# Building a quarter of the low weight parts with an accumulating DMA in a split-precision decoder block

## The chip, the cores and the metric

The kernel runs on one core of a Trainium2 chip. The metric is the device time of one execution in microseconds (us). Three executions of the kernel before took 811.44, 811.97 and 812.96 us, so the median is 811.97 us.

## What is computed

The reference is one residual decoder layer on 256 tokens of width 2048, all in float32. Cut to what matters here:

```python
h = rms_norm(x, g_mix)
u, z_ssm, c_q, k, v, z_attn, k_idx, w_idx, gate_ssm, gate_attn = split(h @ w_in)
o_ssm  = (s5_scan(u) * silu(z_ssm)) @ w_ssm_out
o_attn = (topk_attention(c_q, k, v, k_idx, w_idx) * silu(z_attn)) @ w_attn_out
x = x + (sigmoid(gate_ssm) * o_ssm + sigmoid(gate_attn) * o_attn) @ w_o
x = x + sigmoid(rms_norm(x, g_ple) @ w_ple_gate) * rms_norm(p @ w_ple, g_ple_post)
return rms_norm(x, g_final)
```

Nearly all of the work is matrix products of the 256 token rows with large weight matrices, which are read once from HBM.

## The kernel before, in words

A float32 product is made from three products of reduced-precision operands (type float32r). Each operand is split into a high part (the value rounded) and a low part (the value minus its high part), and the kernel adds high x high, high x low and low x high in PSUM. For the activations this is done once per stage. For the weights it is done for each piece as it comes in.

The weights come in **units** of 128 partitions x 1024 columns (512 KB; eight units of the v/key projection have 672 columns). There are 256 units, numbered 0 to 255, and the main loop takes one per step. For each unit:

- `issue_unit` (L88) loads it from HBM into a tile `raw` by a DMA on the SP queue (L99). There are 5 `raw` buffers (L94), so a load has to wait until the unit five before it has been used up.
- `unit_hi` (L243) makes `hi`, the rounded copy, on ACT (L252). There are 4 `hi` buffers.
- `unit_lo` (L255) makes `lo = raw - hi` on DVE (L264). There are 4 `lo` buffers.
- TensorE then does 24 matmuls of 256 columns or 12 of 512 columns with `hi` and `lo` (L142).

At step s the loop issues the matmuls of unit s, then `hi` of unit s+3, then whatever work was deferred to this step, then `lo` of unit s+2, then the load of the next unit not yet loaded (unit s+5), and then `pump` (L229) lets generator threads run up to a budget. Since four buffers are in turn, `hi` and `lo` of unit u reuse the buffers of unit u-4 and cannot start before the matmuls of unit u-4 are done. Five units are loaded ahead of the loop by `first_loads` (L112).

Beside the units, threads do the rest of the layer. Those that matter below:

- `s5_tables` (from L754) and `s5_powers` (L732) prepare tables for the state-space branch. GpSimd (POOL) does 49 small products of 128x32 (L738 to L744) and six large ones of 128x1024 (L775 to L777); DVE does large products at L767 to L771. In the program text the POOL work stands behind the last of the DVE products.
- `s5_gen` (from L820) runs the scan on DVE, with matmuls into the PSUM tile `aux`.
- `attn_gen` does indexer, top-k and attention.

POOL otherwise computes a few small powers for the norms and a few masks. It issues no DMA. The framework sets all semaphores itself and also orders the instructions of each engine by a plan of its own, so that an engine's order can differ from the program text: the memset of `kb` (L805), which stands late in the text, is among the first things POOL runs.

Of the kernel before, what the change touches and what calls it, by code (L numbers as in the profile page):

```python
# [10 lines left out]
F32R = mybir.dt.float32r  # L11
I32 = mybir.dt.int32
AF = mybir.ActivationFunctionType
ALU = mybir.AluOpType
# [4 lines left out]
P = 128  # L19
# [14 lines left out]
XLAG = 1  # L34
ULATE = 4
TRLAG = 2

C_U, C_ZS, C_CQ, C_K, C_V, C_ZA, C_KI, C_GS, C_GA = 0, 1024, 2048, 2560, 2816, 3072, 4096, 4176, 6224

# [5 lines left out]
def block_kernel(ctx: ExitStack, tc: tile.TileContext, A: dict, out: bass.AP):  # L45
    nc = tc.nc
    V, S, G, PE = nc.vector, nc.scalar, nc.gpsimd, nc.tensor
# [3 lines left out]
    wp = ctx.enter_context(tc.tile_pool(name="wp", bufs=4))  # L51
# [8 lines left out]
    def nm(s):  # L60
        uid[0] += 1
        return f"{s}_{uid[0]}"

    def slot(tag, shape, dt=F32):
        return cp.tile(shape, dt, tag=tag, name=nm(tag))
# [18 lines left out]
    raws = {}  # L84
    dma_next = [0]
    chunks = []

    def issue_unit(between=None):  # L88
        n = dma_next[0]
        if n >= len(units):  # L90
            return
        c, h, cols = units[n][:3]
        kind, idx = chunks[c]
        r = wp.tile([P, 1024], F32, tag="raw", name=nm("raw"), bufs=5)  # L94
        src = (A["wts"][idx] if kind == "w" else A["wvk"][idx])[:, h * cols:(h + 1) * cols]
        q = 2 if between else 1
        for i in range(q):
            s = slice(i * cols // q, (i + 1) * cols // q)
            nc.sync.dma_start(r[:, s], src[:, s])  # L99
            if between and i == 0:  # L100
                between()
        raws[n] = r
        dma_next[0] += 1
# [83 lines left out]
    units = []  # L187
# [3 lines left out]
    def defer(n, fn):  # L191
        deferred.append((step[0] + n, fn))

    def run_deferred(flush=False):
        while True:
            due = [d for d in deferred if flush or d[0] <= step[0]]
            if not due:
                return
            for d in due:
                deferred.remove(d)  # L200
            for d in due:
                d[1]()
# [26 lines left out]
    def pump(budget):  # L229
        credit[0] = min(credit[0] + budget, 3.0)  # L230
        while credit[0] > 0:
            ready = [t for t in threads if t[1] <= step[0]]
            if not ready:
                return
            credit[0] -= advance(ready[0])

    def drain(t):
        while not t[2]:
            advance(t)

    his, los = {}, {}

    def unit_hi(u):  # L243
        if u >= len(units):
            return
        cols = units[u][2]
        hi = wp.tile([P, 1024], F32R, tag="hi", name=nm("hi"))
        src = raws[u][:, :cols]
        q = 2 if u < 3 else 1
        for i in range(q):  # L250
            o = slice(i * cols // q, (i + 1) * cols // q)
            S.copy(hi[:, o], src[:, o])  # L252
        his[u] = hi

    def unit_lo(u):  # L255
        if u >= len(units):
            return
        cols = units[u][2]
        lo = wp.tile([P, 1024], F32R, tag="lo", name=nm("lo"))
        src = raws.pop(u)  # L260
        q = 2 if u < 3 else 1
        for i in range(q):
            o = slice(i * cols // q, (i + 1) * cols // q)
            TT(lo[:, o], src[:, o], his[u][:, o].bitcast(F32), ALU.subtract)  # L264
        los[u] = lo
# [118 lines left out]
    u = slot("S5", [P, 8, T])  # L384
# [189 lines left out]
    def to_channels(src, nb, done):  # L574

        ps = aux_ps()
        for h in range(2):
            for b in range(4):
                o = (b % 2) * T + h * P
                transpose(ps[:, b // 2, o:o + P], src[:, h, nb * CW + b * P:nb * CW + (b + 1) * P], ident)  # L580
        done(ps.rearrange("p a (b t) -> p (a b) t", b=2))

    def ev_ao(nb):
# [5 lines left out]
        def f(h, ps):  # L589
# [9 lines left out]
            if h == 1:  # L599
                defer(TRLAG, lambda: to_channels(R["os"], nb, tr))  # L600
        return f

    def ev_o(nb):
# [9 lines left out]
        def f(h, ps):  # L613
# [8 lines left out]
            if h == 1:  # L622
                defer(TRLAG, lambda: to_channels(R["x2"], nb, tr))
                if nb == NC - 1:
# [468 lines left out]
    for i in range(NWARM):  # L1093
        mm(wps[:, :T], warm[:, :P], warm)
    unit_hi(0)
    xprep(0)
    unit_lo(0)
    xprep(1)
    unit_hi(1)
    unit_lo(1)  # L1100
    unit_hi(2)
    NU = len(units)
    for s in range(NU):
        step[0] = s
        fn, need = units[s][3:]
        for n in need or ():
            if callable(n):
                n()
            else:
                run_deferred()  # L1110
                drain(R[n])
        fn(his.pop(s), los.pop(s))
        unit_hi(s + 3)
        run_deferred()
        unit_lo(s + 2)
        issue_unit()
        pump(BUDGET)
# [117 lines left out]
```

## Time and profile before

| | |
|---|---|
| median of three executions | 811.97 us |
| the profiled execution, its own time | 811.61 us |
| span of its trace | 809.8 us |
| mean granted TensorE clock | 0.986 |
| bytes read from HBM | 147.79 MB |

The profile gives busy time for each engine: PE is TensorE's matmuls, PEld its weight loads, DVE VectorE, ACT ScalarE, POOL GpSimd, SP the engine that issues most DMAs. A view of waits says which instruction an engine stood idle for. A timeline lists one engine's instructions in order of time. Times inside the trace are in us from the start of the span; the execution's own time is 1.8 us longer than its span.

### The profile page before, as it was taken

The numbers are of one execution on the slowest core, as the hardware profiler recorded it, in microseconds if no ns is written. First come the engines' busy times: TensorE is split into PE (matmuls) and PEld (weight loads), VectorE is DVE, ScalarE is ACT, GpSimd is POOL, SyncE is SP. The second block draws the span as 40 slices with busy tenths as digits, with TensorE's granted clock in tenths as the row PEclk, the third lists the DMA queues.
The fourth block names the chain that finished last, engine by engine and source line by source line (L and its number), as shares of the span: only waits on it lengthen the run. The fifth ranks groups of instructions, "written<-read, shape, count | busy, mean of one in ns | idle before, by whom it ended". The sixth has DMA issues, their size and how long they took to land.

```text
span 809.8 us, 12802 instructions
## 1 busy us (share of the span) xinstructions
PE 783.5 (97%) x5020; PEld 676.5 (84%) x5020; DVE 575.1 (71%) x834; ACT 393.9 (49%) x536; POOL 72.7 (9%) x77
## 2 busy tenths in 40 slices
PE   6899999999999999999999999999999999999993
PEld 5899997887999887799999987887887888888882
DVE  6999656999645999664669877666688555556662
ACT  6354544544566454463445474535445444445542
POOL 4369900000000000000000000000000000000000
PEclk7999999999999999999999999999999999999997
DMA  8576854656745655734754546676767665555522
GB/s 288 182 261 193 270 192 141 201 177 210 260 135 176 194 184 182 252 121 129 243 183 156 194 162 226 224 238 199 268 202 236 224 204 185 184 182 181 184 79 104
DMA packets 52061, 158.07 MB, mean 195 GB/s; under 512 B 5920, under 2 KB 12064, under 8 KB 51616
## 3 DMA queue, kind: packets, MB, share of 16 engines
q1 hardware_dynamic: 47392, 150.96, 57.2%
q10 hardware_dynamic: 4608, 6.29, 2.2%
q8 instruction: 39, 0.64, 0.3%
q14 instruction: 22, 0.18, 0.1%
HBM read 147.79 MB, written 8.39 MB: 193 GB/s over the span
## 4 chain that ended last, share of the span: by engine, by line
PE 36%; issue 11%; DMA 1%; DVE 1%; ACT 1%; ACTq 0%; POOLq 0%; POOL 0%; DVEq 0%
PE main L142 33%; PE aux L142 2%; PE aux L150 1%; DMA zld<-za_d 1%; DVE lo L264 0%; ACT hi L252 0%; DMA raw<-in_wts_dram 0%; DVE S L1022 0%; ACT S L1127 0%; ACTq L1230 0%; ACT S L586 0%; DVE t L980 0%; POOLq L1230 0%; POOL r_c L633 0%; ACT S L1023 0%
## 5 line engine op out<-in xcount | busy, mean ns | idle before, releaser
L252 ACT CAST hi<-raw 128x1024 fp32r<-128x1024 f32 (+2 forms) x259 | 266.4, 1031 | 363.7 <-PE main L142 318.3
L264 DVE TENSOR_TENSOR lo<-raw,hi 128x1024 fp32r<-128x1024 f32 (+2 forms) x259 | 316.5, 1225 | 154.6 <-ACT hi L252 154.0
L142 PE MATMUL main<-hi,S 128*128 128x512 f32 x544 | 175.3, 397 | 0.9 <-ACT S L1023 0.9
L142 PE MATMUL main<-hi,XH 128*128 128x512 f32 (+1 forms) x416 | 163.1, 392 | 0.0
L142 PE MATMUL main<-lo,XH 128*128 128x512 f32 (+1 forms) x416 | 162.4, 390 | 0.4 <-DVE lo L264 0.4
L142 PE MATMUL main<-hi,XL 128*128 128x512 f32 (+1 forms) x416 | 161.9, 389 | 0.0
L142 PE MATMUL main<-XH,hi 128*128 128x256 f32 x448 | 127.5, 285 | 0.0
L142 PE MATMUL main<-XH,lo 128*128 128x256 f32 x448 | 126.2, 282 | 0.0
L142 PE MATMUL main<-XL,hi 128*128 128x256 f32 x448 | 126.1, 282 | 0.0
L142 PEld LDWEIGHTS main<-hi,S 128*128 128x128 f32 x544 | 102.2, 188 | 25.2 <-ACT S L1023 1.6
L142 PE MATMUL main<-lo,S 128*128 128x512 f32 x272 | 107.9, 397 | 0.0
L142 PEld LDWEIGHTS main<-lo,XH 128*128 128x128 f32 x416 | 78.1, 188 | 18.8 <-DVE lo L264 1.9
L142 PEld LDWEIGHTS main<-hi,XH 128*128 128x128 f32 x416 | 78.1, 188 | 18.0
L142 PEld LDWEIGHTS main<-hi,XL 128*128 128x128 f32 x416 | 78.1, 188 | 17.3
L142 PEld LDWEIGHTS main<-XH,hi 128*128 128x128 f32 x448 | 84.8, 189 | 0.6
L142 PEld LDWEIGHTS main<-XH,lo 128*128 128x128 f32 x448 | 84.8, 189 | 0.0
L142 PEld LDWEIGHTS main<-XL,hi 128*128 128x128 f32 x448 | 84.7, 189 | 0.0
L142 PE MATMUL main<-S,hi 128*128 128x256 f32 x384 | 69.3, 283 | 0.1
L142 PEld LDWEIGHTS main<-S,hi 128*128 128x128 f32 x384 | 58.9, 188 | 1.7 <-issue 1.0
L142 PEld LDWEIGHTS main<-lo,S 128*128 128x128 f32 x272 | 51.2, 188 | 11.0
L142 PE MATMUL main<-S,lo 128*128 128x256 f32 x192 | 53.8, 280 | 0.0
L142 PEld LDWEIGHTS main<-S,lo 128*128 128x128 f32 x192 | 36.2, 188 | 0.0
(213 smaller groups left out, 687.0 us busy)
## 6 DMA issues: line engine op xcount, KB each, us to landing
raw<-in_wts_dram SPq DMA_DIRECT2D x247, 512.0 KB, 4.0
raw<-in_wvk_dram SPq DMA_DIRECT2D x8, 336.0 KB, 2.9
gs_d<-big ACTq DMA_DIRECT2D x8, 256.0 KB, 3.9
ga_d<-big ACTq DMA_DIRECT2D x8, 256.0 KB, 4.0
big<-gs_d SPq DMA_DIRECT2D x8, 256.0 KB, 4.3
big<-ga_d SPq DMA_DIRECT2D x8, 256.0 KB, 3.8
S<-in_grow_dram SPq DMA_DIRECT2D x2, 1024.0 KB, 7.7
big<-in_xtok_dram SPq DMA_DIRECT2D x8, 256.0 KB, 3.9
```

The lines of the kernel that those rows point to most:

```text
L142: PE.matmul(o, l, r, start=start, stop=stop, **kw)
L150: PE.matmul(o, i, idn, is_transpose=True)
L252: S.copy(hi[:, o], src[:, o])
L264: TT(lo[:, o], src[:, o], his[u][:, o].bitcast(F32), ALU.subtract)
```

## The change

For every fourth unit from unit 12 on that has 1024 columns (`by_dma`), DVE's subtraction is left out. In its place ACT writes minus the rounded weights into the `lo` tile, and a DMA issued by GpSimd reads the same weights from HBM a second time and adds them onto that tile. This is started at step s for unit s+4 (`unit_ahead`), where the subtraction was placed at step s for unit s+2. There are 59 such units: 61 multiples of four from 12 to 252, less two of the narrow ones. Apart from that, two more loads are issued ahead of the main loop, so that the load issued at step s is that of unit s+7. The numbers of buffers stay as they are.

```diff
+DLO0 = 12
+DLON = 4
...
+    def by_dma(u):
+        return u >= DLO0 and u % DLON == 0 and units[u][2] == 1024
+
+    def unit_ahead(u):
+
+        if u >= len(units) or not by_dma(u):
+            return
+        c, h, cols = units[u][:3]
+        lo = wp.tile([P, 1024], F32R, tag="lo", name=nm("lo"))
+        S.activation(lo, raws[u], AF.Copy, scale=-1.0)
+        src = A["wts"][chunks[c][1]][:, h * cols:(h + 1) * cols]
+        nc.gpsimd.dma_start(lo, src, accum_op=ALU.add)
+        los[u] = lo
+
     def unit_hi(u):
...
         cols = units[u][2]
+        if by_dma(u):
+            raws.pop(u)
+            return
         lo = wp.tile([P, 1024], F32R, tag="lo", name=nm("lo"))
...
     unit_hi(2)
+    for i in range(2):
+        issue_unit()
     NU = len(units)
...
         unit_hi(s + 3)
+        unit_ahead(s + 4)
         run_deferred()
```

## Rows read from the trace of the kernel before

**Rows 1.** The page, busy time and share of the span of each engine
```profile
PE 783.5 (97%) x5020; PEld 676.5 (84%) x5020; DVE 575.1 (71%) x834; ACT 393.9 (49%) x536; POOL 72.7 (9%) x77
```

**Rows 2.** Waits of PE: who waited for whom, total us, times, longest us
```profile
PE aux L142 <- DVE lo L264: 3.3, 2, 3.1
PE aux L142 <- issue: 1.6, 1, 1.6
...
PE main L142 <- ACT S L1023: 0.9, 1, 0.9
PE main L142 <- DVE lo L264: 0.4, 2, 0.2
PE aux L150 <- DVE t L980: 0.2, 1, 0.2
```

**Rows 3.** The page's groups of instructions: the high part and the low part
```profile
L252 ACT CAST hi<-raw 128x1024 fp32r<-128x1024 f32 (+2 forms) x259 | 266.4, 1031 | 363.7 <-PE main L142 318.3
L264 DVE TENSOR_TENSOR lo<-raw,hi 128x1024 fp32r<-128x1024 f32 (+2 forms) x259 | 316.5, 1225 | 154.6 <-ACT hi L252 154.0
```

**Rows 4.** ACT's timeline, the casts of units 12, 15, 16 and 19: start, us
```profile
46.71 1.05 ACT L252 CAST hi<-raw 128x1024 fp32r<-128x1024 f32 x1 [1.79 <-PE main L142]
...
55.19 1.06 ACT L252 CAST hi<-raw 128x1024 fp32r<-128x1024 f32 x1 [1.43 <-PE main L142]
58.03 1.05 ACT L252 CAST hi<-raw 128x1024 fp32r<-128x1024 f32 x1 [1.78 <-PE main L142]
...
66.55 1.05 ACT L252 CAST hi<-raw 128x1024 fp32r<-128x1024 f32 x1 [1.78 <-PE main L142]
```

**Rows 5.** DMA: the loads of the units, a load twice as large, the queue's share
```profile
raw<-in_wts_dram SPq DMA_DIRECT2D x247, 512.0 KB, 4.0
...
S<-in_sb_dram SPq DMA_DIRECT2D x1, 1024.0 KB, 7.5
...
DMA to landing us min/median/max: 2.8/4.0/10.5
...
q1 hardware_dynamic: 47392, 150.96, 57.2%
```

**Rows 6.** SP: its timeline (one issue), and its waits for a free buffer
```profile
42.89 0.33 SPq L99 DMA_DIRECT2D raw<-in_wts_dram  x1
...
SPq L99 <- DVE lo L264: 480.4, 198, 5.6
```

**Rows 7.** POOL's timeline: start, us, instruction, idle time before it
```profile
0.86 0.95 POOL L805 MEMSET kb<- 128x1024 f32 x1
...
45.67 0.24 POOL L738 TENSOR_TENSOR sp_er<-abar 128x32 f32<-128x32 f32 x1 [9.86 <-DVE abar L683]
...
52.55 1.28 POOL L740 TENSOR_TENSOR pre<-sp_eq,sp_er 128x32 f32<-128x32 f32 x1
...
83.67 1.92 POOL L775 TENSOR_TENSOR S<-S,abar 128x1024 f32<-128x1024 f32 x1
...
98.03 2.41 POOL L777 TENSOR_TENSOR S<-S,S 128x1024 f32<-128x1024 f32 x1
```

**Rows 8.** Stages: us, busy of PE, PEld, DVE, ACT, POOL; clock, DMA share, GB/s
```profile
45.70:98.00 52.30, 52.30 (x446) 52.30 (x446) 43.73 (x51) 25.00 (x30) 48.64 (x54) 1.00 0.77 239
...
490.00:600.00 110.00, 109.82 (x512) 89.02 (x511) 74.19 (x118) 51.21 (x74) 0.58 (x2) 1.00 0.70 231
```

**Rows 9.** DVE's timeline: two low parts, and the last large product
```profile
24.08 4.52 DVE L264 TENSOR_TENSOR lo<-raw,hi 128x1024 fp32r<-128x1024 f32 x2
...
73.45 1.22 DVE L771 TENSOR_TENSOR S<-S,S 128x1024 f32<-128x1024 f32 x1
```

**Rows 10.** PE's timeline around its longest wait
```profile
27.52 0.39 PE L142 MATMUL aux<-XH,lo 128*128 128x256 f32 x1 [3.09 <-DVE lo L264]
29.18 0.42 PE L142 MATMUL aux<-XH,lo 128*128 128x256 f32 x1
29.40 0.42 PE L142 MATMUL aux<-XH,hi 128*128 128x256 f32 x1
...
32.33 0.28 PE L142 MATMUL main<-XL,hi 128*128 128x256 f32 x1
32.45 0.28 PE L142 MATMUL main<-XH,lo 128*128 128x256 f32 x1
```

## The prediction, made before the changed kernel was run

> **What bounds the kernel now.** I read the engines' busy shares first: PE is busy 97% of the span, DVE 71%, ACT 49%, POOL 9% [rows 1]. Then PE's waits, because a relieved engine pays only where PE stood still for it. The longest, 3.1 us for a `lo`, lies at 24 to 27 us, before the changed units begin; of the later ones I count 1.6 + 0.9 + 0.4 + 0.2 = 3.1 us [rows 2]. So TensorE is the bound, and DVE's subtractions are almost wholly beside it. Third, the spacing of ACT's casts: the cast of unit u starts when PE has finished unit u-4, so the casts of units 12 to 16, from 46.71 to 58.03, give PE's pace there, 2.83 us per unit [rows 4]. Last, the stages: from 45.7 to 98 us POOL is busy 48.64 of 52.3 us, and the DMA engines 77% [rows 8]. After that POOL is almost idle.
>
> **What is removed.** 59 subtractions of 1.225 us, 72 us of DVE [rows 3]. PE cannot start earlier for most of it; the ceiling of the gain is the 3.1 us above. I take 0.
>
> **What is added on ACT.** 59 casts of 1.03 us, 61 us on an engine busy 394 of 810 us [rows 1, 3]. The new cast reuses the `lo` buffer of unit u-4, so it waits for PE to end that unit, as `hi` of unit u does. What stands behind it on ACT, that `hi` (1.05 us later) and deferred evacuations, has two units of PE work or more as cover. If that cover were gone, each would cost its 1.05 us. I take 0.
>
> **The two loads ahead.** With five `raw` buffers a load still waits for the unit five before it: SP already stands 480 us in such waits, 198 times [rows 6]. The loads cannot start sooner; only their rank against other DMAs on SP rises (gates, attention inputs). A displaced one would be late by at most a unit, 2.8 us, and has several units before its use. I take 0.
>
> **The accumulating DMA, in the steady state.** Its deadline comes from the casts: it can begin when PE ends unit u-4 (46.71 for unit 12) and PE starts unit u when it ends u-1 (55.19): 8.48 us [rows 4]. The chain is the cast, 1.05 us, POOL's issue, and the transfer. No row shows POOL issuing a DMA: it is bounded by SP's issue, 0.33 us [rows 6], and by a small POOL instruction slowed beside DVE, 1.28 us [rows 7]; I take 0.7. No row shows an accumulation: below, it lands like a plain 512 KB load, 4.0 us in the median (2.8 at best); above, since the old tile must be read too, like a load of twice the bytes, 7.5 us [rows 5]. Its bytes lie between the two, so I take the middle, 5.75. That gives 1.05 + 0.7 + 5.75 = 7.5 us against 8.48, so it is hidden by 1.0 us; the ends are 5.4 us (hidden) and 9.85 us (1.4 us late, 59 times: 81 us).
>
> The Trainium skill speaks against the change here: SBUF — State Buffer, section "SBUF: two separate sides", says that GpSimd cannot write the descriptors of its DMAs while VectorE runs an instruction in a 2-port mode, and that such a DMA took about 3100 ns in place of 620. By it the transfer would be about 2.5 us longer (an estimate from that page), 10 us in all and 1.5 us late each time, some 90 us. The same page's section "Who interferes with whom" says that a VectorE instruction with two SBUF inputs, as the subtraction is, holds up only GpSimd's reads.
>
> **DMA load.** The SP queue's 150.96 MB took 57.2% of the engines' time [rows 5], 1.6 us per 512 KB. 59 more tiles at once to twice that are 94 to 190 us, 12 to 23 points on average. In the fullest late stage, 70% [rows 8], some 9 such tiles in 110 us bring it to 83 to 96%. That still fits, and I take 0 beyond the transfer's longer end above.
>
> **The first three DMAs behind POOL's tables.** This is the term that decides my number. POOL runs its instructions in a fixed order, and the order is the framework's plan, not the text: the memset of `kb` stands at 0.86 us, and the powers start at 45.67 us although the text puts them behind the product at 73.45 [rows 7, 9]. Where the plan puts the DMAs of units 12, 16 and 20 this trace cannot show. At best each goes as soon as its cast is done (0 us); at worst behind all the table work, which ends at 98.03 + 2.41 = 100.4 us [rows 7]. I take a plan that counts a small POOL product at its undisturbed 0.24 us (it really takes up to 1.28 beside DVE [rows 7]).
> - Unit 12: the cast ends at 47.76, 2.09 us after POOL's start, so behind nine products; the tenth begins at 52.55 [rows 4, 7]. 52.5 + 6.45 (issue and transfer) = 58.95 against 55.19: PE stands 3.8 us.
> - Unit 16: planned at 59.08, 13.4 us after the start, behind 49 x 0.24 = 11.8 us of small products and one large. Really these end at 83.67 + 1.92 = 85.6 us [rows 7]; with PE standing from 66.55 + 3.8 = 70.35 on, DVE runs dry and the 21 small products left take perhaps 0.4 us in place of 0.65, so 80.5. It lands at 86.9: PE stands 16.6 us. (Without that speeding-up 21.7, behind everything 36.5.)
> - Unit 20: planned 24.8 us after the start, behind the large products too (six of some 2.4 us): 93.5, landing at 99.95, against 86.9 + 4 x 2.84 = 98.3: 1.7 us.
>
> After a wait of 3.1 us PE ran at a spacing of 0.22 us in place of 0.12 from 29.2 to 32.2 us, some 14 matmuls: 1.3 us lost at the lower of its two levels, 1.2 GHz, before it was back at 2.4 [rows 10]. Two long waits: 2.6 us.
>
> **Sum.** 3.8 + 16.6 + 1.7 + 2.6 = 24.7 us on the profiled execution's 811.61 us (its span of 809.8 and 1.8 around it): 836.3. The median lies 0.36 us higher, so 836.7; I say **836 us**.
>
> **Rivals.**
> 1. *Late every time.* The transfer lies near its upper end, or POOL's issue has to wait out DVE instructions (1.28 - 0.24 = 1.04 us for each [rows 7]; two make 9.6 us). PE then waits before every fourth unit. For it: DMA engines at 70 to 77% in the fullest stages [rows 8] and DVE at 71% [rows 1]; against it: a margin of 1.0 us and PE's slack of one matmul. Half-way to the upper end, 0.7 us late 59 times, it costs 41 us: 878 us with the early waits; at the end, 81 us: 918. This is also where the skill's rule on descriptors points; the small products stretched beside DVE agree with some blocking, while no run here shows it for a DMA.
> 2. *Nothing to be seen.* The plan puts the first DMAs well and each later one lands in time. For it: every other term is covered; against it: 48.6 us of POOL work in the way. 812 us.
> 3. *Faster.* As rival 2, and the relieved DVE brings the scan and attention steps earlier, so that PE's waits after 30 us go: 812 - 3.1 = 809 us. The place is the 1.6 us wait in the scan's `aux` matmuls [rows 2]; it decides if these are reached before PE. Against it: that wait is put down to "issue", not to DVE, and it needs all three early DMAs on time.
> 4. *The plan holds POOL's tables back for the DMAs.* Then the scan starts late. Some 25 us (unit 12's to unit 20's cast) would be lost if the scan has no slack: 837 us, the same sign.
>
> **How the numbers follow.** A change within 0.2% (1.6 us) cannot be told from none. Chances: my forecast 0.45, rival 1 0.26, rival 2 0.15, rival 3 0.08, rival 4 0.06. So faster 0.08, same 0.15, slower 0.77. The range goes from 809 (rival 3) to 890: this takes in my own upper cases (3.8 + 36.5 us and the clock, some 855) and rival 1 up to about 0.9 us late each time; left out are its upper end and what lies below. The forecast's own range is 815 to 856.
>
> **What would show it.** Right: PE waits before units 12, 16 and perhaps 20 for a DMA onto `lo`, one of them over 10 us, with POOL still in its tables; PE's granted clock falls behind them; after 110 us no PE wait on such a DMA; DVE busy about 503 us, ACT about 455. The copies' landing time near 5.75 us. Wrong: PE waits on `lo` spread over all 59 units (rival 1), or none at all with POOL's table work interrupted at 48 us (rivals 2 and 3), or an accumulation that lands in 4 us or takes more than 8.

## The result, and the profile after

The changed kernel takes 867.29 us (median of 4 runs, 865.77 to 871.87) against 812.47 us of the kernel before on the same chip (4 runs): a ratio of 1.0682 [1.0638, 1.0727], 54.8 us slower, where 24 us had been forecast. The profiled execution took 867.73 us, its span is 865.6 us, and the mean granted clock fell from 0.986 to 0.960.

First the page: busy time of each engine, the granted clock in 40 slices, and the chain that ended last by engine.

```profile
PE 799.3 (92%) x5020; PEld 686.3 (79%) x5020; DVE 501.9 (58%) x775; ACT 444.3 (51%) x595; POOL 114.4 (13%) x136
...
PEclk6995999999999999999999999999999999998998
...
PE 60%; DMA 12%; DVE 10%; issue 8%; ACT 5%; POOL 4%; SPq 0%; ACTq 0%; POOLq 0%; DVEq 0%
```

Against [rows 1], DVE lost 73 us (72 forecast) and ACT gained 50 (61 forecast). What matters is PE: the same 5020 matmuls kept it busy for 15.8 us more (799.3 - 783.5), and outside them it stood 66.3 us (865.6 - 799.3) in place of 26.3. 15.8 and 40.0 are the whole 55.8 us by which the span grew. The clock dips in the fourth slice (65 to 87 us), where PE stood, and now and then later; the short dips are below what a slice of 22 us shows, and come further down. In the chain, DMA has 12%; on the page of before it had 1%.

The page's groups for the changed units:

```profile
L268 ACT CAST hi<-raw 128x1024 fp32r<-128x1024 f32 (+2 forms) x259 | 262.9, 1027 | 200.3 <-PE main L144 170.0
L283 DVE TENSOR_TENSOR lo<-raw,hi 128x1024 fp32r<-128x1024 f32 (+2 forms) x200 | 239.1, 1202 | 156.8 <-ACT hi L268 109.7
...
L254 ACT ACTIVATE lo<-raw 128x1024 fp32r<-128x1024 f32 x59 | 62.5, 1060 | 162.2 <-DMA raw<-in_wts_dram 137.8
...
L256 POOL DMA_DIRECT2D lo<-in_wts_dram x59 | 51.3, 870 | 643.6 <-ACT lo L254 575.0
```

L254 is the new negating cast, L256 the accumulating DMA; L268 and L283 are the high and the low part of [rows 3]. In [rows 3] ACT's idle time ahead of `hi` was PE's doing, 318.3 us: ACT was early and waited for a buffer. Now that is 170.0 us, and the new cast has an idle time of a new kind: 137.8 us in which ACT stood still for the load of a `raw` tile.

The waits of PE (total us, times, longest us), to be held against [rows 2]:

```profile
PE main L144 <- DMA lo<-in_wts_dram: 22.3, 4, 18.7
PE main L144 <- ACT big L449: 5.1, 3, 2.2
PE main L144 <- DVE lo L283: 3.7, 5, 1.9
PE main L144 <- ACT S L662: 3.6, 1, 3.6
```

All rows of this view add up to 52.6 us (13.1 before). The accumulating DMAs have 22.3 of it, in four waits: one of 18.7 us, and three of 0.79 to 1.39 us at 424, 520 and 570 us. The rest is many short waits for ACT and DVE: for a PSUM tile not yet evacuated (`big`), a low part, a scan or attention tile.

**Where the long wait lies.** POOL's timeline (start, us, instruction, idle time before it and its cause):

```profile
42.87 1.04 POOL L256 DMA_DIRECT2D lo<-in_wts_dram  x1 [7.34 <-ACT lo L254]
44.62 0.23 POOL L757 TENSOR_TENSOR sp_er<-abar 128x32 f32<-128x32 f32 x1 [0.71 <-DVE abar L702]
...
76.19 3.78 POOL L794 TENSOR_TENSOR S<-S,abar 128x1024 f32<-128x1024 f32 x2
79.91 0.89 POOL L256 DMA_DIRECT2D lo<-in_wts_dram  x1
...
89.55 0.88 POOL L256 DMA_DIRECT2D lo<-in_wts_dram  x1
```

Unit 12's DMA went out before the tables began. Unit 16's stood behind all the small products and two large ones, and went out at 79.91; its cast, the L254 at 54.86 on ACT's timeline (shown further down), had been done 24 us before. Unit 20's went out at 89.55, behind the last of the large products. PE's timeline at that place:

```profile
85.32 0.58 PE L144 MATMUL main<-XH,lo 128*128 128x256 f32 x1 [18.74 <-DMA lo<-in_wts_dram]
85.70 0.41 PE L144 MATMUL main<-XH,hi 128*128 128x256 f32 x1
85.91 0.41 PE L144 MATMUL main<-XL,hi 128*128 128x256 f32 x1
...
89.49 0.28 PE L144 MATMUL main<-XH,hi 128*128 128x256 f32 x1
89.61 0.28 PE L144 MATMUL main<-XL,hi 128*128 128x256 f32 x1
```

PE stood 18.74 us. Behind that its matmuls start 0.21 us apart, the pace of the lower level (1.2 GHz), until 89.3; at 89.49 they are back at 0.12.

**Where the rest lies.** The stages (us, busy of PE, PEld, DVE, ACT, POOL; granted clock, DMA share, GB/s):

```profile
45.00:102.00 57.00, 38.26 (x308) 38.06 (x307) 31.59 (x39) 19.53 (x21) 43.71 (x57) 0.82 0.61 174
102.00:200.00 98.00, 97.35 (x724) 84.03 (x723) 63.18 (x99) 51.13 (x64) 6.01 (x7) 1.00 0.80 231
550.00:620.00 70.00, 64.22 (x291) 51.49 (x290) 35.03 (x56) 34.14 (x58) 4.06 (x5) 0.98 0.83 251
```

In the first stage PE stood 18.7 us. In later ones it was idle too, by less (5.8 of 70 us from 550 on), with the DMA engines at 0.80 to 0.83, where the fullest late stage in [rows 8] had 0.70.

ACT's timeline shows what such a loss is made of:

```profile
201.30 1.06 ACT L254 ACTIVATE lo<-raw 128x1024 fp32r<-128x1024 f32 x1 [6.99 <-DMA raw<-in_wts_dram]
202.27 2.93 ACT L268 CAST hi<-raw 128x1024 fp32r<-128x1024 f32 x3
...
212.60 1.06 ACT L254 ACTIVATE lo<-raw 128x1024 fp32r<-128x1024 f32 x1 [5.90 <-DMA raw<-in_wts_dram]
213.56 1.03 ACT L268 CAST hi<-raw 128x1024 fp32r<-128x1024 f32 x1
214.50 0.68 ACT L449 ACTIVATE big<-main,r_c 128x512 f32<-128x512 f32 x1
```

ACT stands 6.99 us for a load; three casts of high parts follow in a row, without a wait of their own. Then it stands 5.90 us, and behind the new cast and one `hi` comes an evacuation, at 214.50, for which PE is already waiting:

```profile
215.23 0.50 PE L144 MATMUL main<-hi,XH 128*128 128x512 f32 x1 [2.09 <-ACT big L449]
```

So the wait that PE shows names `big`, the evacuation; its cause is the load that ACT waited for two instructions earlier. And it costs more than its 2.09 us. The same columns as for the stages, around it:

```profile
213.00:215.23 2.23, 0.14 (x1) 0.00 (x0) 2.20 (x3) 2.18 (x3) 0.86 (x1) 1.00 0.67 231
215.23:219.00 3.77, 3.77 (x10) 2.95 (x11) 2.75 (x3) 2.68 (x3) 0.00 (x0) 0.56 0.84 156
219.00:222.00 3.00, 3.00 (x14) 2.43 (x13) 0.00 (x0) 0.72 (x1) 0.00 (x0) 0.98 1.06 344
```

After the stand the granted clock is 0.56 for 3.77 us, which is some 3.3 us at the lower level, then full again: 10 matmuls ran where 17 or so would have at the pace behind it (14 in 3.0 us), some 1.6 us more. Over stretches of 20 us, the clock from 100 us on was 0.91 in five of them, from 200, 320, 420, 580 and 640 us, and 0.83 in one, from 780, else 0.94 or more: 5 x 1.8 + 3.4 = 12 us of full clock withheld, where before no such stretch between 40 and 780 us was under 1.00. With the early spell that is most of the 15.8 us by which PE was busy for longer. This stand thus cost nearly twice its length. Not every one does: the six spells lie behind PE's waits of 2.09, 2.22, 2.27, 2.34, 2.44 and 3.64 us, while behind those of 1.39 us at 520 and at 570 us, of 2.06 us at 586 and of 1.92 us at 749 the granted clock stayed at 1.00 for the 5.7 us or more that followed.

How the cast comes to stand there is in the order of ACT's instructions (here around units 16 and 20):

```profile
52.12 1.06 ACT L268 CAST hi<-raw 128x1024 fp32r<-128x1024 f32 x1 [1.79 <-PE main L144]
54.86 1.06 ACT L254 ACTIVATE lo<-raw 128x1024 fp32r<-128x1024 f32 x1 [1.69 <-DMA raw<-in_wts_dram]
...
58.32 1.98 ACT L268 CAST hi<-raw 128x1024 fp32r<-128x1024 f32 x2
...
63.43 1.05 ACT L268 CAST hi<-raw 128x1024 fp32r<-128x1024 f32 x1 [1.78 <-PE main L144]
64.58 1.07 ACT L254 ACTIVATE lo<-raw 128x1024 fp32r<-128x1024 f32 x1
66.27 1.05 ACT L268 CAST hi<-raw 128x1024 fp32r<-128x1024 f32 x1 [0.63 <-PE main L144]
```

Counted from the start, these are `hi` of unit 14, the new cast of unit 16, `hi` of units 15 and 16, `hi` of unit 18, the new cast of unit 20, `hi` of unit 19. The source puts the cast of unit u behind the `hi` of unit u-1. The framework's plan puts it earlier: here behind the `hi` of unit u-2, and over the 59 casts behind that of unit u-3 in 36 places, of unit u-2 in 19, and as in the source in four. The earlier the place, the more ACT waited there for the unit's own load: 28 of the 36 waited, 128.4 us in all, 4 of the 19, 9.4 us, and none of the four.

### The profile page after: what moved, and what is told of

Read it like the earlier page. It is cut to its first block, busy times and chain, and to the rows that moved or that the text cites. A ratio compares the mean times of both kernels' runs of the same rounds, so it can differ in the third digit from the quotient of the medians.

```text
span 865.6 us, 12980 instructions
## 1 busy us (share of the span) xinstructions
PE 799.3 (92%) x5020; PEld 686.3 (79%) x5020; DVE 501.9 (58%) x775; ACT 444.3 (51%) x595; POOL 114.4 (13%) x136
## 3 DMA queue, kind: packets, MB, share of 16 engines
q0 software_dynamic: 8496, 30.94, 21.2%
## 4 chain that ended last, share of the span: by engine, by line
PE 60%; DMA 12%; DVE 10%; issue 8%; ACT 5%; POOL 4%; SPq 0%; ACTq 0%; POOLq 0%; DVEq 0%
PE main L144 54%; DMA raw<-in_wts_dram 8%; PE aux L144 5%; DVE lo L283 4%; DMA lo<-in_wts_dram 3%; ACT hi L268 2%; DVE S L884 1%; DVE S L878 1%; DVE S L882 1%; PE aux L152 1%; DMA S<-in_xT_dram 1%; DVE XL L381 1%; ACT XH L626 1%; DMA zld<-za_d 1%; DVE S L880 1%
## 5 line engine op out<-in xcount | busy, mean ns | idle before, releaser
L268 ACT CAST hi<-raw 128x1024 fp32r<-128x1024 f32 (+2 forms) x259 | 262.9, 1027 | 200.3 <-PE main L144 170.0
L283 DVE TENSOR_TENSOR lo<-raw,hi 128x1024 fp32r<-128x1024 f32 (+2 forms) x200 | 239.1, 1202 | 156.8 <-ACT hi L268 109.7
L144 PE MATMUL main<-hi,XH 128*128 128x512 f32 (+1 forms) x416 | 165.8, 399 | 8.8 <-ACT big L449 5.1
L144 PE MATMUL main<-lo,XH 128*128 128x512 f32 (+1 forms) x416 | 164.4, 395 | 2.7 <-DMA lo<-in_wts_dram 1.4
L144 PE MATMUL main<-hi,XL 128*128 128x512 f32 (+1 forms) x416 | 164.1, 394 | 0.0
L254 ACT ACTIVATE lo<-raw 128x1024 fp32r<-128x1024 f32 x59 | 62.5, 1060 | 162.2 <-DMA raw<-in_wts_dram 137.8
L144 PE MATMUL main<-XH,lo 128*128 128x256 f32 x448 | 126.8, 283 | 18.7 <-DMA lo<-in_wts_dram 18.7
L256 POOL DMA_DIRECT2D lo<-in_wts_dram x59 | 51.3, 870 | 643.6 <-ACT lo L254 575.0
L144 PEld LDWEIGHTS main<-XH,hi 128*128 128x128 f32 x448 | 85.3, 190 | 0.7
L144 PEld LDWEIGHTS main<-XL,hi 128*128 128x128 f32 x448 | 85.3, 190 | 0.0
```

What stands on the lines that cost most here:

```text
L144: PE.matmul(o, l, r, start=start, stop=stop, **kw)
L254: S.activation(lo, raws[u], AF.Copy, scale=-1.0)
L256: nc.gpsimd.dma_start(lo, src, accum_op=ALU.add)
```

## The experiments

Two theories for the loss that is spread over the kernel, called A and B in the expectations: by A it comes from the place of the cast on ACT, which waits there for a load and holds up what is queued behind it; by B from the traffic, an extra transfer every fourth unit that makes loads and copies late. Ratios are to runs of the kernel before on the same chip.

**The early DMAs left out** (units 12 to 28 get their low part from DVE again):

```diff
-DLO0 = 12
+DLO0 = 32
```

> The accumulating DMAs begin with unit 32, behind the tables that GpSimd builds until about 90 us; all else as in the changed kernel. Theory (early term): the one wait of 18.7 us on the DMA of unit 16 and the half clock behind it (14.7 us, worth some 7) go, so 867 falls to 840 to 847 us, and no wait of PE on such a DMA is over 2 us. The rest of the loss, about 30 us against the kernel before, stays, and ACT's negating cast still stands some 100 us or more for raw loads. Rival (the early wait is given back later, since another term bounds the stage behind it): 860 us or more.

845.15 us, 1.0411 [1.0362, 1.0461]. Its waits of PE for the DMA, and of ACT for loads:

```profile
PE main L144 <- DMA lo<-in_wts_dram: 1.6, 2, 0.9
```

```profile
ACT lo L254 <- DMA raw<-in_wts_dram: 127.9, 30, 6.8
```

The long wait is gone and 22 us with it (867.3 - 845.2). It was the early term. (The half clock behind it was shorter than the 14.7 us of the expectation: PE ran 4.1 us at it, from 85.3 to 89.4, and lost some 2.) Some 32 us stay, and in them PE hardly waits for the accumulating DMA: 1.6 us over 54 transfers. "Late every time" is ruled out; ACT's wait for loads is nearly as long as before.

**The two loads ahead alone:**

```diff
-DLO0 = 12
+DLO0 = 9999
```

> Only the two loads ahead of the loop; no unit is made by the DMA. With five raw buffers the loads wait for the same buffers as before: 811 to 814 us, SP's waits on lo near 480 us. Rival (the higher rank of the loads holds up the gate and attention inputs on SP): 816 us or more, with PE waits on evacuations of the gates or on the scan of zld.

812.86 us, 1.0000 [0.9989, 1.0012]; SP's waits on `lo` are 478.8 us (480.4 in [rows 6]). They neither cost nor gain.

**The cast alone**, where it stands, without the DMA; DVE adds `raw` to the negated high part where it subtracted, so that the low part is the same:

```diff
-DLO0 = 12
+DLO0 = 32
...
-        src = A["wts"][chunks[c][1]][:, h * cols:(h + 1) * cols]
-        nc.gpsimd.dma_start(lo, src, accum_op=ALU.add)
         los[u] = lo
...
-            raws.pop(u)
+            TT(los[u], raws.pop(u), los[u].bitcast(F32), ALU.add)
```

> From unit 32 on ACT writes minus the rounded weights as in the changed kernel, but DVE adds the raw weights to it where it subtracted before; no accumulating DMA, no second read. Theory A (the negating cast stands on ACT ahead of two hi casts, waits for its raw load and holds them up): ACT still waits over 60 us for raw loads before it, and the time is 820 to 840 us. Theory B (the extra traffic makes all transfers late, and that starves the casts): ACT's wait for raw loads is under 30 us and the time 811 to 815 us.

824.51 us, 1.0144 [1.0102, 1.0186]: some 12 us slower (8 to 15; two executions) with no extra byte moved.

```profile
ACT lo L254 <- DMA raw<-in_wts_dram: 65.7, 20, 6.0
```

ACT waits for loads 65.7 us, although these land in 4.2 us in the median (4.0 before). So the wait needs no extra traffic; the cast's place is enough. But it is half of what the change has from unit 32 on.

**The traffic alone, first try.** All low parts by DVE; POOL adds two half units to a scratch tile that nothing reads:

```diff
+    scr = const("scr", [P, 512], F32R)
...
+        for i in range(2):
+            nc.gpsimd.dma_start(scr, src[:, 512 * i:512 * i + 512], accum_op=ALU.add)
```

> DVE makes every low part as before; from unit 32 on GpSimd issues, for every fourth unit, two accumulating DMAs of half its weights each onto a scratch tile of 512 columns that nobody reads (the t buffers are 7 in place of 9 to make room). The same bytes pass as in the changed kernel, without the negating cast. Theory A: 811 to 817 us, the raw loads land in about 5 us. Theory B: 830 us or more, with PE waits on lo and evacuations spread over the kernel.

1020.95 us, 1.2561, far off every expectation, for a reason of the experiment's own:

```profile
POOL scr L257 <- DMA scr<-in_wts_dram: 423.1, 105, 8.4
...
PE small L144 <- POOL rcq_c L169: 193.7, 1, 193.7
```

Nothing paced these DMAs, each only waited for the last one on the same tile, and the plan queued them on POOL ahead of two tiny powers that PE needs. It says nothing on A or B, but it shows the early term's mechanism from the other side: there a DMA waits behind POOL's arithmetic, here the arithmetic behind DMAs.

**The cast one place later**, asked for behind the `hi` of unit u-1 and one step later:

```diff
-DLO0 = 12
+DLO0 = 32
...
+        unit_ahead(s + 3)
         unit_hi(s + 3)
-        unit_ahead(s + 4)
```

> As the run from unit 32 on (845 us), but the negating cast of unit u is placed at step u-3 ahead of that unit's own hi cast, where it stood ahead of the hi casts of units u-1 and u. Theory A (the early place of the cast on ACT is what lets the late loads through to PE): ACT's waits for raw loads before that cast fall from 128 to under 50 us and the time to 815 to 832 us; the DMA has less time (about 8.5 us for cast, issue and landing of 1.06 + 0.87 + 5.8 = 7.7 us), so PE may wait up to 1 us on some of them, some 10 us in all. Theory B (the traffic alone): the time stays within 5 us of 845.

828.95 us, 1.0210 [1.0183, 1.0238]; in the order of ACT's instructions the casts now stand about one `hi` later, behind that of unit u-2 (31 of the 54) or u-1 (23).

```profile
ACT lo L254 <- DMA raw<-in_wts_dram: 22.2, 7, 4.2
...
PE main L144 <- DMA lo<-in_wts_dram: 7.0, 5, 3.0
```

ACT's wait for loads falls from 127.9 to 22.2 us and the loss from 33 to 17: theory A. The seven waits that are left are all at places behind u-2. But the DMA now starts later, and PE waits for it 7.0 us.

**A sixth `raw` buffer**, the cast where it was; room is made by fewer buffers of the tile `t`:

```diff
-DLO0 = 12
+DLO0 = 32
...
-        r = wp.tile([P, 1024], F32, tag="raw", name=nm("raw"), bufs=5)
+        r = wp.tile([P, 1024], F32, tag="raw", name=nm("raw"), bufs=6)
...
-            t = etmp("t", bufs=9)
+            t = etmp("t", bufs=5)
...
```

> As the run from unit 32 on (845 us), with six raw buffers in place of five, so that the loads can in fact start one unit earlier (the t buffers are 5 in place of 9 to make room). Theory A: ACT's waits for raw loads fall from 128 to some 40 to 80 us, the time to 820 to 835 us. Theory B: the loads are late by bandwidth, so one unit more of lead helps little: 838 us or more.

819.53 us, 1.0096 [1.0062, 1.0129], just under the lower end expected by A.

```profile
ACT lo L254 <- DMA raw<-in_wts_dram: 46.9, 15, 4.4
```

The same instructions and the same bytes, loads that may run one unit further ahead (they land in 5.5 us, 5.4 without the sixth buffer), and of 33 us only 8 are left.

**Both of these together** (the two diffs above):

> Both together: the cast ahead of its own hi, and six raw buffers with 5 t buffers. Theory A: ACT's waits for raw loads before the cast are nearly gone (under 20 us), the time is 811 to 822 us and what is left are waits on the DMA itself. Theory B: over 830 us.

825.08 us, 1.0164 [1.0146, 1.0183], a miss: slower than the sixth buffer alone. ACT does not wait for loads ahead of the cast any more, but PE waits 4.4 us in three waits for the DMA, which lands in 7.2 us in the median. With the load in time, the earlier cast is the better one: there PE waited 0.7 us for the DMA. That these 3.7 us and the clock behind them are the whole 5.5 us of difference is not shown.

**The traffic alone, paced**: one DMA of a whole unit onto a scratch tile, started by a cast of one column of the last high part; all low parts by DVE:

```diff
-        lo = wp.tile([P, 1024], F32R, tag="lo", name=nm("lo"))
-        S.activation(lo, raws[u], AF.Copy, scale=-1.0)
+        S.activation(scr[:, 0:1], his[u - 1][:, 0:1].bitcast(F32), AF.Copy)
...
-        nc.gpsimd.dma_start(lo, src, accum_op=ALU.add)
-        los[u] = lo
+        nc.gpsimd.dma_start(scr, src, accum_op=ALU.add)
```

> DVE makes every low part as before; for every fourth unit from 32 on GpSimd issues one accumulating DMA of its 512 KB onto a scratch tile that nobody reads, paced by a cast of one column on ACT that follows the hi cast of unit u-1 (5 t buffers make room). The traffic of the changed kernel, without its cast that waits for a raw load. Theory A: 811 to 818 us although raw loads land in over 5 us. Theory B: 830 us or more.

819.53 us, 1.0092 [1.0077, 1.0108]: 7.5 us, between the two expectations, much nearer A's.

**The same with a plain DMA** (`nc.gpsimd.dma_start(scr, src)`):

> The paced traffic run (819.5 us, landing in 7.8 us) with plain DMAs onto the scratch tile in place of accumulating ones: the same bytes from HBM without the old tile being read. If the accumulation is what loads the DMA engines: landing 5 to 6 us, the raw loads land in under 5.0 us, time 812 to 816 us. If the second read of the weights alone does it: landing over 7 us and 818 us or more.

815.0 us, 1.0033 [1.0019, 1.0048]. The queue's row and the issues on the page, first with accumulation, then without:

```profile
q0 software_dynamic: 7776, 28.32, 20.0%
...
L257 POOL DMA_DIRECT2D scr<-in_wts_dram x54 | 47.2, 874 | 592.8 <-ACT scr L255 575.2
...
scr<-in_wts_dram POOLq DMA_DIRECT2D x54, 512.0 KB, 7.8
```

```profile
q0 software_dynamic: 7776, 28.32, 12.8%
...
L257 POOL DMA_DIRECT2D scr<-in_wts_dram x54 | 29.1, 538 | 605.9 <-ACT scr L255 588.0
...
scr<-in_wts_dram POOLq DMA_DIRECT2D x54, 512.0 KB, 5.5
```

For the same 28.32 MB the accumulating DMAs hold the engines 20.0% of 817.7 us, 3.03 us for each of the 54, the plain ones 12.8% of 814.0, 1.93 us. Of the 7.5 us that the traffic costs, reading the weights a second time is nearly 3 and accumulating some 5.

**The sixth buffer without the DMAs**, a control for the room made (`DLO0 = 9999`, six `raw`, five `t`):

> Control for the runs with room made: six raw buffers, 5 t buffers, the two loads ahead, and no unit made by the DMA. If the room made (5 t buffers) costs nothing and the sixth raw buffer gains nothing where TensorE is the bound: 811 to 814 us, so that the 7 us left in the runs with 5 t buffers are the extra traffic's. If the 5 t buffers are what those 7 us are: 817 us or more.

811.36 us, 0.9991 [0.9978, 1.0004]. Fewer `t` buffers cost nothing, and the sixth `raw` gains nothing by itself: it only takes back what the change spends.

**Unit 16 left to DVE**, all others as in the change:

```diff
-        return u >= DLO0 and u % DLON == 0 and units[u][2] == 1024
+        return u >= DLO0 and u != 16 and u % DLON == 0 and units[u][2] == 1024
```

> The changed kernel with unit 16 alone made by DVE again; units 12 and 20 stay with the DMA. Theory (any DMA issued by GpSimd while it builds the tables comes out behind them): the long wait moves to unit 20, 10 to 22 us, and the time stays at 860 to 868 us. Rival (the long wait belongs to unit 16 alone): 843 to 848 us.

868.70 us, 1.0694 [1.0613, 1.0774] (two executions), just over the end expected; the wait is not gone but moved to unit 20:

```profile
PE main L144 <- DMA lo<-in_wts_dram: 21.9, 4, 19.7
```

On POOL the DMAs of units 20 and 24 go out together at 92.42, behind the last large product. Not a certain unit is at fault, but the place among the tables that the plan gives to these DMAs.

**The whole change with the sixth buffer** (`DLO0 = 12`):

> The changed kernel with units 12 to 28 too, and six raw buffers (5 t buffers). If the wait behind GpSimd's tables and the casts held up by late loads are two separate terms that add: some 22 us above the run with six buffers from unit 32 on (819.5), so 838 to 846 us, with one wait of PE of 15 to 20 us on the DMA of unit 16 and no other over 3 us. Rival (the sixth buffer also shortens the early wait, since that wait came from the raw loads): under 830 us.

837.18 us, 1.0326 [1.0272, 1.0380], just under the 838 to 846 expected. All of PE's waits for the accumulating DMA are one, longer than the 15 to 20 us expected:

```profile
PE main L144 <- DMA lo<-in_wts_dram: 22.2, 1, 22.2
```

Against the same kernel from unit 32 on (819.53) the early DMAs cost 18 us, against 22 with five buffers: the two losses add up, nearly. No version made here beats the kernel before.

What each leaves on PE, from the page and the waits of the profiled executions, in us (waits: all rows of PE's view):

| kernel | span | PE's waits | PE busy |
|---|---|---|---|
| before | 809.8 | 13.1 | 783.5 |
| after | 865.6 | 52.6 | 799.3 |
| after, from unit 32 on | 840.9 | 33.6 | 793.0 |
| cast alone | 819.9 | 21.6 | 785.0 |
| cast one place later | 829.5 | 24.5 | 790.7 |
| six `raw` buffers, from unit 32 on | 821.2 | 18.6 | 788.3 |
| traffic alone, paced | 817.7 | 17.7 | 786.2 |

## Why the prediction was right in part

**Right.** The direction, and that the early loss comes from POOL's plan. The term of unit 16 is the forecast's almost to the step: issue at 80.5 forecast, 79.91 in the trace (behind two large products, where one was forecast); landing 86.9 and 85.3; PE's wait 16.6 and 18.7 us. Leaving the early DMAs out is worth 22 us. DVE's time (503 forecast, 502 measured) and ACT's (455 and 444) came out, and no gain from DVE's relief is to be seen, as argued. The DMA's chain did as well: an issue of 0.7 was taken and is 0.87 us; for the transfer 5.75 was taken, and the landing times of the 59 (least, median, most) are

```profile
DMA to landing us min/median/max: 5.3/5.6/9.8
```

So its steady state is hidden: PE waited for a copy four times, not 59. Three of these came after 110 us, where none was forecast. The margin of 1.0 us was not tested by this: the casts stand earlier than the forecast had them, which gave the copies more time. With the later cast, where copies land in 6.6 us, the chain is 1.06 + 0.86 + 6.6 = 8.5 us against the forecast's deadline of 8.48, and there PE waits five times.

The rule of the Trainium skill that was weighed (SBUF — State Buffer, "SBUF: two separate sides") is that a DMA of GpSimd took about 3100 ns in place of 620 while VectorE kept it from writing descriptors. Applied as in the prediction, it would have made the DMAs late each time. No such delay is seen: the 59 issues, in a kernel that still has 200 subtractions on DVE, took 856 to 1045 ns, with a median landing of 5.6 us. The rule itself, which is on VectorE instructions in a 2-port mode, is not tested by this: no view here tells whether one ran beside these DMAs.

**Wrong within the early term.** Unit 12's 3.8 us did not come: its cast ran at 41.48, not at 46.71, and its DMA was ahead of the tables. Unit 20's 1.7 us did not come either. The clock's 1.3 us for a wait became some 1.8 behind the long one (about 19 matmuls at a spacing of 0.21 in place of 0.12). These errors nearly cancel: that the forecast's 24.7 us for the early term came so near to the 22 measured is in part luck.

**The step that failed** is the paragraph "What is added on ACT", taken at 0. It rested on one sentence: that the new cast reuses the `lo` buffer of unit u-4 and so waits for PE to end that unit, as the `hi` of unit u does. It does not: unit 12's cast ran at 41.48, when PE had not ended unit 8 (the `hi` of unit 12, which waits for that, ran at 46.45), and unit 20's at 64.58, before PE had begun unit 16. The plan found it a place one or two `hi` casts earlier than the source in 55 of 59 cases. There its own load has often not landed (32 waits, 137.8 us), and what ACT holds behind it, two or three high parts and the evacuations, comes late. In place of 0 this cost 12 us by itself and, with the traffic, up to 25 of the 33 us spread over the kernel, as much as a sixth `raw` buffer took back. I had priced the cast's 1.05 us behind PE's lead, not a wait that it could bring with it, and I had asked what is queued around a new instruction only for the DMA on POOL. The sentence "the loads cannot start sooner" was right [rows 6], and was the warning: a tile that is loaded just in time for `hi` of unit u is not there two or three units before.

The second term at 0, "DMA load", failed with it, by less: the share did grow by what was worked out (21.2% for the 59 copies, 12 to 23 points forecast), but "that still fits" was not 0; the traffic alone cost 7.5 us:

```profile
q0 software_dynamic: 8496, 30.94, 21.2%
...
raw<-in_wts_dram SPq DMA_DIRECT2D x247, 512.0 KB, 5.4
```

The loads land in 5.4 us where they took 4.0 [rows 5], and with the sixth buffer, where they land as late, most of the loss was gone. The parts: cast alone 12 us, traffic alone 7.5, both 33, and with a sixth buffer in front of both 8, which is about the traffic's own. As I read it, the cast's place turns late loads into stalls of ACT, the traffic makes them late, and the stalls hold back the high and low parts that free the `raw` buffers of the next loads; this last turn of the circle is argued, not measured.

**What stays open.** That the pair costs 14 us more than its two parts is measured (33 against 12 + 7.5). By the table above, the loss from unit 32 on is 20.5 us of PE's waits and 9.5 us of busy time, the clock behind them; which of the waits come from ACT's stalls and which from late low parts on DVE was followed through for one only, that at 215.23. One rival for a part of it was not tried: an early cast also holds one of the four `lo` buffers for longer, and from unit 32 on DVE's subtractions waited 24.0 us for PE to free theirs, where the kernel before shows no such wait; a fifth `lo` buffer would tell. It is not the larger part, since the sixth `raw` buffer took back 25 of 33 us with four `lo` buffers (these waits are 15.2 us there). Why the plan puts the cast so early was seen in the order alone, not tried.

## What to carry to other kernels

Look up where the framework's plan puts a new instruction on its in-order engine, and what it waits for there: the 1 us that it takes is the smaller price, and the load that it waits for is charged to everything behind it, here with some 12 us of lower clock behind six of PE's waits on top. When work is moved ahead, the buffers that feed it must run ahead as far: one more `raw` buffer took back 25 of 33 us. And a DMA issued on a queue that also does arithmetic can be late by that arithmetic, here by 24 us, while the DMA engines had a share of only 0.61.

## What was not expected of the hardware

An accumulating DMA of 512 KB holds the DMA engines 1.57 times as long as a plain one from the same queue (3.03 and 1.93 us), lands 2.3 us later beside the same work (7.8 and 5.5), and takes POOL 0.87 us to issue in place of 0.54. And the time that TensorE worked at its lower level behind a stand hardly differed between three stands: 4.1 us behind 18.7 us of standing, some 3.3 behind 2.09, some 3.0 behind 3.1 [rows 10]. For each us of standing the short waits that had such a spell were thus dearer than the long one; four others of 1.39 to 2.06 us had none.
